# Norms between stages: sums of squares and residual adds moved to VectorE, in a two-layer hybrid trunk

## The chip, the core and the metric

The kernel runs on one core of a Trainium2 chip. The metric is the device time of one execution in microseconds (us); smaller is better. Before the change three runs took 1175.69, 1177.09 and 1179.84 us, a median of 1177.09 us.

The engines have short names throughout: PE is TensorE (matrix products), DVE is VectorE, ACT is ScalarE, POOL is GpSimd, SP is SyncE, which issues most DMAs. Each engine works through its own list of instructions in a fixed order; semaphores make it wait for others.

## The reference

The reference is a decoder trunk of two layers on 512 tokens of 1024 features. Each layer has a mixer (layer 0: dilated attention beside a state-space layer; layer 1: a gated linear recurrence) and a SwiGLU feed-forward network (FFN) with 2816 hidden columns. Every one of the four sub-layers stands between two norms:

```
def rms_norm(x, g):
    x32 = x.astype(jnp.float32)
    y = x32 * lax.rsqrt(jnp.mean(x32 * x32, axis=-1, keepdims=True) + NORM_EPS) * g.astype(jnp.float32)
    return y.astype(x.dtype)
...
        x = x + rms_norm(mix, norm_mix_post[layer])
        hn = rms_norm(x, norm_ffn_pre[layer])
        ff = swiglu(hn, ffn_w_gate[layer], ffn_w_up[layer], ffn_w_down[layer])
        x = x + rms_norm(ff, norm_ffn_post[layer])
```

So at each boundary between two sub-layers a sub-layer's output is normed and added to the residual x, and the new x is normed again, which needs the sum of its squares over the 1024 features of each token. There are three such boundaries: layer 0's mixer to its FFN, that FFN to layer 1's mixer, layer 1's mixer to its FFN.

## The kernel before

**Tiling.** Everything is held feature-major: a tile is 128 features x 512 tokens, and x is eight such tiles, `xT[0]` to `xT[7]`. A product in fp32 accuracy is made of three passes (`mm3`): operands are split into a high part (`xh`, `whi_*`) and the rest (`xl`, `wlo_*`), and high x high, high x low and low x high are added up in PSUM. Weights come from HBM as `wraw_*`; ACT rounds the high part (L240), DVE subtracts for the low part (L241).

**A boundary** is the end of `out_proj` (from L413), called three times: with the name `mo0` (first boundary, around 255 to 300 us in the trace), `fd0` (around 610 to 660) and `mo1` (around 780 to 830). In the trace `mo0` and `mo1` both show as `_mo`. The 512 tokens are done in two halves, h = 0 and 1, of 256 tokens (`HT`). For each half:

- The last products of the projection end (`op_*`), DVE adds them to the output tiles o (L527), ACT squares (L528), DVE adds the squares (L530), and PE sums them over features by one-column matmuls against a tile of ones (`cs_*`). DVE (L378) and POOL (L381, a power) make the reciprocal root `rst`/`rsy`, and PE spreads it over partitions (`bc_*`).
- Then `norm_half(h)` goes over the eight feature tiles f. For each: DVE scales o by gain and row (L494, a SCALAR_TENSOR_TENSOR, with two tensor inputs and a per-partition scalar); x is increased by it (on DVE at L498 for f < `NDVE` = 1, on POOL at L500 for the other seven); ACT makes `xh` (L501) and the square of the new x (`nsq_*`, L504); DVE makes `xl` (L489).
- The squares are summed on PE (`next_sums`, L472): for each feature tile and each block of 128 tokens one matmul with the 128 x 128 block of squares as weights and one column of ones as data, 16 in each half, accumulated in PSUM over the eight tiles (`ns_*`).

**Beside the norm** PE runs `half_cols(h)`: the first four column blocks ("heads") of the next stage, which take feature tile f as soon as its `xh` and `xl` are there: 12 products of 256 columns for each f and half (tiles `mo0b`, `f00b` and so on). The sums of the new squares are wanted only after that, in `mid()`: the next stage's products use the un-normed x, and the row of reciprocal roots is applied to their results (`rst_f`, `bc_f`, `bcs_f`).

**The order of the work.** Steps of `norm_half` are generators in a heap, taken when a clock that counts the cost of the issued products reaches their due time (`NORM_CS`, `NORM_BC`, `NORM_F` = 1000 ns for each feature tile). PE, DVE and ACT instructions of this part keep the order in which the program is written (`keep_in_program_order`, through `pe.pin` and `seq_of`); all other instructions are ordered by the framework's scheduler, so a change here can shift the order elsewhere too.

**After an FFN boundary** the feed-forward starts with column pairs that are computed with fewer products (a Strassen-like scheme). It needs sums and differences of weights (`wraw_s_f`, `wraw_t_f`, L642 to L645 on DVE) and of x (`xa_f`, `xb_f` on ACT at L660 and L661, differences `wraw_tr_f` on DVE at L664 to L667, then high parts `th_f` on ACT and low parts `tl_f` on DVE at L671 and L672). Pairs 02 to 21 go through tiles `f00b` to `f03b`; the first two of them, 02 and 03, wait for these differences. After the `fd0` boundary no such scheme follows: the next stage (`xb`, `gg`) uses plain products.

## Time and profile before

| | us |
|---|---|
| median of 3 runs | 1177.09 |
| the profiled execution | 1173.47 |
| its span in the trace | 1171.5 |
| outside the span (1173.47 - 1171.5) | 1.97 |

The profile shows one execution on the chip. A row of a group view reads: line, engine, operation, output <- inputs, count, then durations in ns (least/median/greatest) or busy time. Durations of following instructions on one engine overlap, since each starts before the one ahead has fully left the pipeline; how far apart two instructions start (the pitch) is therefore taken from start times in the timeline, and is shorter than a duration. A window row gives the busy time of each engine in a stretch of time, in us, with the number of rows, then the granted PE clock (1.00 is full speed) and DMA figures. An fp32 matmul leaves two rows in the trace, a product of the split parts one.

The busy shares over the span are 97% for PE, 75% for DVE, 54% for ACT and 5% for POOL; DVE's share in the norms and after them differs a lot from that mean.

### The profile page before, as it was taken

To read this page: it belongs to the slowest core of one execution; us is meant where nothing else is said; L and a number is where in the kernel's file an instruction comes from. 1 tells how busy PE (TensorE), PEld (TensorE's weight loads), DVE (VectorE), ACT (ScalarE), POOL (GpSimd) and SP (SyncE) were. 2 spreads that over 40 slices of the span, in tenths; PEclk is the share of its full clock that TensorE was granted. 3 is DMA by queue.
4 is the path that set the end of the run, shared out by engine and by line. 5 is a ranking of instruction groups with operands and counts; after the bars stand their busy time and mean duration, and the time that the engine had idled before them with its cause. 6 is when DMAs were issued, how large, how long until landed. Compare 5 with 4: busy or idle time off the path is not lost.

```text
span 1171.5 us, 20250 instructions
## 1 busy us (share of the span) xinstructions
PE 1134.0 (97%) x7550; PEld 1013.6 (87%) x7550; DVE 877.7 (75%) x1841; ACT 628.4 (54%) x1290; POOL 60.6 (5%) x101
## 2 busy tenths in 40 slices
PE   7899999999999999999999999999999999999997
PEld 6787766789999999988889987889999999988886
DVE  7978866557999899983445896966999899994224
ACT  6556667446755545662243469744955455582221
POOL 2000010004000000000002200004000000000001
PEclk9899899999999999999999999999999999999999
DMA  8254320430343323333340323340253343233221
GB/s 214 91 149 126 101 75 1 134 101 26 110 118 100 91 82 108 92 122 93 114 120 1 91 91 91 122 129 1 73 144 96 92 119 93 85 123 121 95 63 72
DMA packets 165273, 113.45 MB, mean 97 GB/s; under 512 B 26820, under 2 KB 141752, under 8 KB 165176
## 3 DMA queue, kind: packets, MB, share of 16 engines
q1 hardware_dynamic: 161848, 109.94, 32.1%
q10 hardware_dynamic: 3040, 2.17, 0.7%
q8 instruction: 59, 0.97, 0.4%
q14 instruction: 38, 0.31, 0.1%
q0 software_dynamic: 288, 0.07, 0.0%
HBM read 103.75 MB, written 4.19 MB: 92 GB/s over the span
## 4 chain that ended last, share of the span: by engine, by line
PE 75%; ACT 9%; DVE 7%; DMA 5%; issue 2%; POOL 1%; ACTq 0%; SPq 0%; DVEq 0%; POOLq 0%
PE fo L170 10%; PE op_fd L170 10%; PE op_mo L170 5%; PE f11b L170 4%; PE f12b L170 4%; PE f01b L170 4%; PE f00b L170 4%; PE f10b L170 4%; PE f02b L170 4%; PE qkv L170 4%; PE gg L170 3%; PE f13b L170 2%; PE f03b L170 2%; PE xbb L170 2%; PE fd0b L170 2%
## 5 line engine op out<-in xcount | busy, mean ns | idle before, releaser
L241 DVE TENSOR_TENSOR wlo_fo<-wraw_fo,whi_fo 128x512 fp32r<-128x512 f32 x44 | 30.3, 691 | 63.9 <-PE fo L170 58.3
L170 PE MATMUL op_fd<-hi_f,whi_fd 128*128 128x512 f32 (+1 forms) x200 | 73.6, 368 | 0.0
L170 PE MATMUL op_fd<-lo_f,whi_fd 128*128 128x512 f32 (+1 forms) x200 | 73.2, 366 | 0.0
L170 PE MATMUL op_fd<-hi_f,wlo_fd 128*128 128x512 f32 (+1 forms) x200 | 73.0, 368 | 0.0
L170 PE MATMUL fo<-wlo_fo,hi_f 128*128 128x512 f32 x176 | 69.5, 395 | 0.0
L170 PE MATMUL fo<-whi_fo,lo_f 128*128 128x512 f32 x176 | 69.2, 394 | 0.0
L170 PE MATMUL fo<-whi_fo,hi_f 128*128 128x512 f32 x176 | 68.9, 396 | 0.0
L240 ACT ACTIVATE whi_fo<-wraw_fo 128x512 fp32r<-128x512 f32 x44 | 27.6, 631 | 70.6 <-DMA wraw_fo<-in_ffn_w_down_dram 44.5
L241 DVE TENSOR_TENSOR wlo_fd<-wraw_fd,whi_fd 128x512 fp32r<-128x512 f32 x44 | 30.1, 691 | 46.7 <-ACT whi_fd L240 42.4
L240 ACT ACTIVATE whi_fd<-wraw_fd 128x512 fp32r<-128x512 f32 x44 | 27.4, 629 | 54.9 <-DMA wraw_fd<-in_ffn_w_down_dram 32.6
L170 PEld LDWEIGHTS op_fd<-lo_f,whi_fd 128*128 128x128 f32 x200 | 37.7, 189 | 6.9
L170 PE MATMUL qkv<-whi_qkv,xh_m 128*128 128x512 f32 x96 | 42.3, 442 | 1.4 <-DVE up L1204 1.2
L170 PEld LDWEIGHTS op_fd<-hi_f,wlo_fd 128*128 128x128 f32 x200 | 37.7, 188 | 6.7
L170 PEld LDWEIGHTS op_fd<-hi_f,whi_fd 128*128 128x128 f32 x200 | 37.7, 188 | 6.5
L170 PE MATMUL qkv<-wlo_qkv,xh_m 128*128 128x512 f32 x96 | 39.3, 409 | 2.9 <-DVE wlo_qkv L241 2.9
L170 PEld LDWEIGHTS fo<-whi_fo,lo_f 128*128 128x128 f32 x176 | 33.1, 188 | 7.8
L170 PEld LDWEIGHTS fo<-whi_fo,hi_f 128*128 128x128 f32 x176 | 33.1, 188 | 7.7
L170 PEld LDWEIGHTS fo<-wlo_fo,hi_f 128*128 128x128 f32 x176 | 33.1, 188 | 7.5
L170 PE MATMUL qkv<-whi_qkv,xl_m 128*128 128x512 f32 x96 | 39.3, 410 | 0.0
L642 DVE TENSOR_TENSOR wraw_s_f<-wraw_f,wraw_f 128x512 f32<-128x512 f32 x40 | 27.4, 686 | 12.6 <-DMA wraw_f<-in_ffn_w_up_dram 9.3
L241 DVE TENSOR_TENSOR wlo_mo<-wraw_mo,whi_mo 128x512 fp32r<-128x512 f32 x32 | 21.1, 685 | 15.3 <-ACT whi_mo L240 15.1
L643 DVE TENSOR_TENSOR wraw_t_f<-wraw_s_f,wraw_f 128x512 f32<-128x512 f32 x40 | 27.3, 684 | 6.3 <-DMA wraw_f<-in_ffn_w_gate_dram 6.3
(1975 smaller groups left out, 4301.2 us busy)
## 6 DMA issues: line engine op xcount, KB each, us to landing
wraw_f<-in_ffn_w_gate_dram SPq DMA_DIRECT2D x88, 256.0 KB, 3.2
wraw_f<-in_ffn_w_up_dram SPq DMA_DIRECT2D x88, 256.0 KB, 3.3
wraw_fd<-in_ffn_w_down_dram SPq DMA_DIRECT2D x44, 256.0 KB, 2.8
wraw_fo<-in_ffn_w_down_dram SPq DMA_DIRECT2D x44, 256.0 KB, 3.0
wraw_qkv<-in_ev_w_in_dram SPq DMA_DIRECT2D x24, 256.0 KB, 3.5
wraw_mo<-in_ev_w_out_dram SPq DMA_DIRECT2D x16, 256.0 KB, 4.7
wraw_xb<-in_od_w_in_dram SPq DMA_DIRECT2D x16, 256.0 KB, 2.8
wraw_gg<-in_od_w_in_dram SPq DMA_DIRECT2D x16, 256.0 KB, 2.9
```

What stands on the lines that cost most here:

```text
L170: self.pin(nc.tensor.matmul(o, lhsT=lhsT, rhs=rhs, start=start, stop=stop, **kw))
L240: act.activation(hi, src, AF.Copy)
L241: eng.tensor_tensor(lo, src, hi.bitcast(F32), op=ALU.subtract)
L642: dve.tensor_tensor(s1, a21, a22, op=ALU.add)
L643: dve.tensor_tensor(s2, s1, a11, op=ALU.subtract)
```

## The change

At each of the three boundaries:

- All eight residual adds of a half are done on DVE (L490 in the changed kernel); 14 POOL instructions go for each boundary, 42 in all. POOL keeps the power of L381.
- The squares of the new x are added up on DVE: ACT's squares go to four half-tiles, the first of them is the accumulator (`sq[3]`), and seven DVE additions (L494 and L498 of the changed kernel) bring the other seven in. That is 14 more DVE additions for each boundary, 28 with the residual adds.
- `next_sums` goes. PE makes four one-column matmuls for each boundary in place of 32, written after all products of the heads' first half and `drain()`, with no pinned place; the scheduler puts them.
- The low part `xl` (`split_lo`) of tile f - 1 is made in every step, right behind the scaling of tile f; before, it came one or two tiles later when POOL did the add.

```
-NDVE = 1
...
-        acc2 = [None, None]
+        acc2, total = [None, None], [None, None]
...
-        def next_sums(h, fs, q):
-            for i, f in enumerate(fs):
-                for t in range(2):
-                    c = 2 * h + t
-                    pe.pin(nc.tensor.matmul(nsum[:, c:c + 1], lhsT=q[:, i * HT + t * P:i * HT + (t + 1) * P],
-                                            rhs=ones[:, 0:1], start=(c == 0 and f == 0), stop=(f == NF - 1),
-                                            skip_group_check=True))
...
+            sq = [sb.tile([P, S], F32, tag="sqacc" if h else "sq", bufs=2, name=f"nsq_{nm}{h}{i}") for i in range(2)]
+            sq = [q[:, HS[i]] for q in sq for i in range(2)]
...
-                if late and late[0] < max(NDVE, f - 1):
+                if late:
                     split_lo()
-                if f < NDVE:
-                    seq_of(dve.tensor_tensor(xf, xf, oh, op=ALU.add))
-                else:
-                    pool.tensor_tensor(xf, xf, oh, op=ALU.add)
+                seq_of(dve.tensor_tensor(xf, xf, oh, op=ALU.add))
                 seq_of(act.activation(xh[f][:, HS[h]], xf, AF.Copy, scale=col(gname, glayer * NF + f)))
-                if f % 2 == 0:
-                    q = sb.tile([P, S], F32, tag="sqacc" if h else "sq", bufs=2, name=f"nsq_{nm}{h}{f}")
-                seq_of(act.activation(q[:, HS[f % 2]], xf, AF.Square))
+                seq_of(act.activation(sq[f % 3] if f else sq[3], xf, AF.Square))
+                if f > 1:
+                    seq_of(dve.tensor_tensor(sq[3], sq[3], sq[(f - 1) % 3], op=ALU.add))
                 late.append(f)
-                if f % 2 and f > 1:
-                    next_sums(h, (f - 3, f - 2), qlast)
-                if f % 2:
-                    qlast = q
...
-            next_sums(h, (NF - 2, NF - 1), qlast)
+            seq_of(dve.tensor_tensor(sq[3], sq[3], sq[(NF - 1) % 3], op=ALU.add))
+            total[h] = sq[3]
...
         in_order[0] = False
+        for t in range(NT):
+            pe.matmul(nsum[:, t:t + 1], lhsT=total[t // 2][:, t % 2 * P:(t % 2 + 1) * P], rhs=ones[:, 0:1],
+                      start=True, stop=True)
```

The order of each engine's list shows where this goes. The list of DVE grows from 1827 to 1917 rows, that of POOL shrinks from 107 to 65 and that of PE from 6890 to 6863 (following equal matmuls share a row).

First place, DVE in the first half of the norm at the first boundary. `o_mo` is the scaled output, `xl_mo` the low part, `xT` the residual, `nsq_mo` the squares; before, a step is one scaling and one low part:

```order
L494 SCALAR_TENSOR_TENSOR o_mo_2825<-o_mo_2825,cols,bc_mo_3123 128x256
L489 SCALAR_TENSOR_TENSOR xl_mo_2995<-xT_178,cols,xh_mo_2987 128x256
L494 SCALAR_TENSOR_TENSOR o_mo_2930<-o_mo_2930,cols,bc_mo_3123 128x256
L489 SCALAR_TENSOR_TENSOR xl_mo_2996<-xT_179,cols,xh_mo_2988 128x256
L378 TENSOR_SCALAR rst_mo_3214<-cs_mo_3209 128x2
L494 SCALAR_TENSOR_TENSOR o_mo_2932<-o_mo_2932,cols,bc_mo_3123 128x256
L489 SCALAR_TENSOR_TENSOR xl_mo_2997<-xT_180,cols,xh_mo_2989 128x256
```

The same engine and place in the changed kernel, two steps:

```order
L487 SCALAR_TENSOR_TENSOR o_mo_2825<-o_mo_2825,cols,bc_mo_3123 128x256
L482 SCALAR_TENSOR_TENSOR xl_mo_2996<-xT_179,cols,xh_mo_2988 128x256
L490 TENSOR_TENSOR xT_180<-xT_180,o_mo_2825 128x256
L494 TENSOR_TENSOR nsq_mo_3127<-nsq_mo_3127 128x256
L487 SCALAR_TENSOR_TENSOR o_mo_2930<-o_mo_2930,cols,bc_mo_3123 128x256
L482 SCALAR_TENSOR_TENSOR xl_mo_2997<-xT_180,cols,xh_mo_2989 128x256
L490 TENSOR_TENSOR xT_181<-xT_181,o_mo_2930 128x256
L494 TENSOR_TENSOR nsq_mo_3127<-nsq_mo_3127,nsq_mo_3126 128x256
```

A step has four DVE instructions where it had two, and the low part now follows by one tile.

Second place, PE at the end of the heads at the first boundary. `ns_mo` is the sum of squares, `mo0b` the heads, `f00b` the first pair. Before, such sums stand between the products, for example:

```order
L170 MATMUL mo0b_3159<-xh_mo_2993,wlo_f_1_2947 128x256
L472 MATMUL ns_mo_3002<-ones,nsq_mo_3278 128x1 x4
L170 MATMUL mo0b_3160<-xh_mo_2993,whi_f_1_2958 128x256
L170 MATMUL mo0b_3160<-xh_mo_2993,wlo_f_1_2959 128x256
L170 MATMUL mo0b_3161<-xh_mo_2993,whi_f_1_2970 128x256
```

In the changed kernel the totals of the second half stand here:

```order
L169 MATMUL mo0b_3163<-xh_mo_2993,wlo_f_1_2983 128x256
L169 MATMUL ns_mo_3002<-ones,nsq_mo_3275 128x1 x2
L169 MATMUL mo0b_3160<-xl_mo_3001,whi_f_1_2946 128x256
L169 MATMUL mo0b_3161<-xl_mo_3001,whi_f_1_2958 128x256
L169 MATMUL mo0b_3162<-xl_mo_3001,whi_f_1_2970 128x256
L169 MATMUL mo0b_3163<-xl_mo_3001,whi_f_1_2982 128x256
L169 MATMUL f00b_3606<-xh_mo_2986,whi_f02a_3492 128x256
```

Only the last four products of the heads stand behind the last sums; the totals of the first half stand at the same place of that half.

Third place, DVE some 40 rows after the norm's end at the first boundary, around the last `tl_f` (the low parts of x's differences). Before:

```order
L672 TENSOR_TENSOR tl_f_3603<-wraw_tr_f_0_3596,th_f_3602 128x512
L241 TENSOR_TENSOR wlo_f03c_3753<-wraw_s_f_0_3737,whi_f03c_3752 128x512
L241 TENSOR_TENSOR wlo_f04d_3909<-wraw_f_0_3881,whi_f04d_3908 128x512
L672 TENSOR_TENSOR tl_f_3603<-wraw_tr_f_2_3597,th_f_3602 128x256
L241 TENSOR_TENSOR wlo_f04d_3913<-wraw_f_4_3883,whi_f04d_3912 128x512
```

In the changed kernel:

```order
L662 TENSOR_TENSOR tl_f_3585<-wraw_tr_f_0_3578,th_f_3584 128x512
L633 TENSOR_TENSOR wraw_t_f_0_3869<-wraw_s_f_0_3867,wraw_f_0_3859 128x512
L634 TENSOR_TENSOR wraw_f_0_3863<-wraw_f_0_3859,wraw_f_0_3863 128x512
L240 TENSOR_TENSOR wlo_f04c_3883<-wraw_s_f_0_3867,whi_f04c_3882 128x512
L662 TENSOR_TENSOR tl_f_3567<-wraw_tr_f_2_3561,th_f_3566 128x256
L662 TENSOR_TENSOR tl_f_3585<-wraw_tr_f_2_3579,th_f_3584 128x256
L635 TENSOR_TENSOR wraw_s_f_4_3868<-wraw_f_4_3861,wraw_t_f_0_3869 128x512
```

The last `tl_f` is row 600 of DVE's list before, 48 rows behind the norm's last low part (row 552); it is row 635 after, 59 rows behind that low part (row 576). The weights of pairs 02 and 03 (`wlo_f02*`, `wlo_f03*`) now all stand ahead of it; before, `wlo_f03b` and one part each of `wlo_f03c` and `wlo_f03d` came after it.

## The prediction

> **What bounds the kernel now.** I read the page's head first, then windows of the trace around the three boundaries, then the groups of the lines that the change touches, then waits. The head says that PE is the engine to look at; the windows say where it isn't:
>
> ```profile
> span 1171.5 us, 20250 instructions
> PE 1134.0 (97%) x7550; PEld 1013.6 (87%) x7550; DVE 877.7 (75%) x1841; ACT 628.4 (54%) x1290; POOL 60.6 (5%) x101
> ```
>
> The windows are the heads with the norm at the first boundary (265 to 298.3), the FFN behind it (two rows), the second boundary and its next stage (622.3, 660), the third boundary and its FFN (793.9, 830, 860). The columns are window, length, then busy time of PE, PEld, DVE, ACT and POOL, then the granted clock:
>
> ```profile
> core 0: us, PE busy (x) PEld busy (x) DVE busy (x) ACT busy (x) POOL busy (x), PEclk, DMA share, GB/s
> 260.00:265.00 5.00, 5.00 (x31) 5.00 (x31) 2.22 (x6) 0.69 (x2) 0.71 (x1) 0.66 0.00 0
> 265.00:298.30 33.30, 32.46 (x276) 32.18 (x275) 26.55 (x64) 24.30 (x56) 13.72 (x16) 1.00 0.19 54
> 300.00:320.00 20.00, 17.93 (x145) 17.19 (x144) 20.00 (x39) 15.08 (x31) 0.00 (x0) 1.00 0.31 88
> 320.00:380.00 60.00, 60.00 (x508) 60.00 (x507) 58.91 (x120) 31.32 (x65) 0.00 (x0) 1.00 0.38 109
> 622.30:660.00 37.70, 36.90 (x314) 36.64 (x313) 24.06 (x78) 15.38 (x38) 13.49 (x16) 1.00 0.10 29
> 660.00:710.00 50.00, 50.00 (x222) 40.59 (x220) 41.55 (x72) 34.50 (x55) 0.00 (x0) 1.00 0.34 102
> 793.90:830.00 36.10, 35.34 (x298) 35.08 (x298) 26.76 (x62) 22.62 (x53) 13.54 (x16) 1.00 0.14 41
> 830.00:860.00 30.00, 28.09 (x232) 27.44 (x231) 28.39 (x57) 20.57 (x42) 0.00 (x0) 1.00 0.33 93
> 860.00:880.00 20.00, 19.00 (x156) 18.38 (x155) 20.00 (x42) 12.15 (x25) 0.00 (x0) 1.00 0.38 110
> ```
>
> Three things stand in them. Within the norms PE is the bound: it idles 0.8 us in each, DVE 6.8 to 13.6. Behind the second boundary PE is busy without a gap and DVE has 8.45 us of 50 to spare. But behind the first and the third, where the FFN's first pairs need sums of weights and of x from DVE, DVE is busy all of 300 to 320 and of 860 to 880, and it is PE that idles: 2.07 us in 300 to 320, 1.91 and 1.00 us in 830 to 880. So time saved on PE in a norm is kept at the second boundary, and at the other two only as far as DVE is ready earlier too; and the change gives DVE more work.
>
> **The matmuls removed.** The sums of squares in the first norm, first as busy time (columns: PE, PEld), then one batch in the timeline (start, length), with four products behind it:
>
> ```profile
> 265.00:298.30 33.30, 7.99 (x64) 8.14 (x64) 1.00 0.19 54
> ...
> 274.98 0.95 PE L472 MATMUL ns_mo<-ones,nsq_mo 128*128 128x1 f32 x8
> 275.79 0.48 PE L170 MATMUL mo0b<-xl_mo,whi_f 128*128 128x256 f32 x2
> 276.11 0.29 PE L170 MATMUL mo0b<-xh_mo,whi_f 128*128 128x256 f32 x1
> 276.23 0.28 PE L170 MATMUL mo0b<-xh_mo,wlo_f 128*128 128x256 f32 x1
> ```
>
> Busy time counts the ends that overlap the next product, so I go by starts: eight rows, which are four matmuls, take 275.79 - 274.98 = 0.81 us, 0.20 us each. A boundary loses 32 - 4 = 28 of them: 28 x 0.20 = 5.7 us; the busy time bounds it from above, 7.99 x 28/32 = 7.0 us. A head product takes 276.23 - 276.11 = 0.12 us, so the 12 products of a feature tile and half take 1.44 us.
>
> **The work added to DVE.** The groups are POOL's add, DVE's scaling and low part, and ACT's two steps (least/median/greatest ns); then POOL's adds of the first boundary's second half as one piece; then DVE instructions that follow each other without a gap, 256 and 512 columns wide:
>
> ```profile
> L500 POOL TENSOR_TENSOR xT<-xT,o_mo x28: 724/917/1008, 266.8 to 819.3; 128x256 f32<-128x256 f32 x28
> L494 DVE SCALAR_TENSOR_TENSOR o_mo<-o_mo,cols,bc_mo x32: 466/471/482, 263.7 to 818.7; 128x256 f32<-128x256 f32 x32
> L489 DVE SCALAR_TENSOR_TENSOR xl_mo<-xT,cols,xh_mo x32: 471/560/912, 266.6 to 823.4; 128x256 fp32r<-128x256 f32 x32
> L501 ACT ACTIVATE xh_mo<-xT,cols x32: 492/509/512, 264.7 to 822.1; 128x256 fp32r<-128x256 f32 x32
> L504 ACT ACTIVATE nsq_mo<-xT x32: 398/401/404, 265.1 to 822.5; 128x256 f32<-128x256 f32 x32
> ...
> 279.92 6.10 POOL L500 TENSOR_TENSOR xT<-xT,o_mo 128x256 f32<-128x256 f32 x7 [4.72 <-DVE o_mo L494]
> ...
> 266.22 0.47 DVE L494 SCALAR_TENSOR_TENSOR o_mo<-o_mo,cols,bc_mo 128x256 f32<-128x256 f32 x1
> 266.61 0.48 DVE L489 SCALAR_TENSOR_TENSOR xl_mo<-xT,cols,xh_mo 128x256 fp32r<-128x256 f32 x1
> ...
> 317.76 0.41 DVE L718 TENSOR_TENSOR pu_f<-pu_f 128x256 f32<-128x256 f32 x1
> 318.10 0.74 DVE L719 TENSOR_TENSOR gt_f<-f00b,bcs_f 128x256 f32<-128x256 f32 x2
> 318.76 0.68 DVE L241 TENSOR_TENSOR wlo_f03c<-wraw_s_f,whi_f03c 128x512 fp32r<-128x512 f32 x1
> 319.36 0.68 DVE L241 TENSOR_TENSOR wlo_f06a<-wraw_f,whi_f06a 128x512 fp32r<-128x512 f32 x1
> ```
>
> By starts a scaling or low part takes 266.61 - 266.22 = 0.39 us, a 256-wide add 318.10 - 317.76 = 0.34 or (318.76 - 318.10)/2 = 0.33, a 512-wide one 319.36 - 318.76 = 0.60. A boundary's 14 residual adds and 14 adds of squares cost DVE 28 x 0.335 = 9.4 us (0.335 lies between the two; with the whole duration of 0.41 us it would be 11.5 us). A step on DVE becomes 0.39 + 0.39 + 0.335 + 0.335 = 1.45 us, beside PE's 1.44 us: level. ACT's step is 0.51 + 0.40 = 0.91 us, and the chain add, xh, low part (0.41 + 0.51 + 0.47 = 1.39 us) fits into a step, so ACT and latency don't set the pace. In the second half POOL now paces the norm at 6.10/7 = 0.87 us a tile, which is faster than PE takes them; the slower DVE pace costs PE nothing as long as DVE starts a half no later than PE.
>
> DVE also gets something back. Low parts take 560 ns beside POOL's adds and 471 without: 14 x 0.09 = 1.2 us. And its waits in the norm:
>
> ```profile
> 263.75:286.20 22.45, 15.66 (x37) 0.99 0.00 1
> ...
> DVE o_mo L494 <- PE bc_mo L170: 4.5, 2, 3.1
> DVE rst_mo L378 <- PE cs_mo L170: 2.0, 1, 2.0
> DVE oacc_mo L530 <- ACT oqs_mo L528: 0.9, 1, 0.9
> DVE xl_mo L489 <- ACT xh_mo L501: 0.7, 2, 0.4
> ```
>
> The first row is DVE from the first scaling to its first FFN instruction: 22.45 - 15.66 = 6.8 us idle, mostly the 3.1 us for the second half's row and the 2.0 us for `cs`. With a fuller list DVE comes to both when they are already there; I leave it the 0.9 us for ACT and some tenths, 1.3 us together. So DVE starts on the FFN's weights later by 9.4 - 1.2 - (6.8 - 1.3) = 2.7 us at the first boundary.
>
> The Trainium skill ("SBUF — State Buffer", section "SBUF: two separate sides") calls the port pair that DVE and GpSimd share an exclusive lock, held for a whole instruction. By that, each POOL add could hold DVE up for its full 0.9 us and 14 of them give back up to 12 us, so DVE would not be late at all and the FFN boundaries would go toward the first rival below. The rows bear out a small part: the scaling, whose row operand lies in PSUM, stays at 471, the low part loses 0.09, and DVE works on through POOL's 6.10 us.
>
> **What becomes of it, boundary by boundary.** *Second* (`fd0`): PE-bound before and behind, so the 5.7 us are kept: -5.7 (-7.0 to -5; a later DVE costs nothing there with 8.45 us spare). *First*: PE ends the heads some 6 to 8 us earlier, and meets a DVE list that runs 2.7 us late. What DVE does last there for pairs 02 and 03 is the last `tl_f`. Before, it started as the first row below shows (a step of the chain that ended last), and the last product of the two pairs as the second:
>
> ```profile
> 311.49 0.34 DVE tl_f L672
> ...
> 323.75 0.28 PE L170 MATMUL f02b<-xh_mo,wlo_f03c 128*128 128x256 f32 x1
> ```
>
> After, DVE's list from the first scaling to that `tl_f` (rows 509 to 635) adds up, with 0.39 and 0.335 for the short ones and 0.60 for the 512-wide, to 52.35 us: 263.75 + 1.3 + 52.35 = 317.4 us. It comes later, but behind the two last `tl_f` PE has only 32 products of these pairs left, 3.8 us: 321.2 us. Before, PE had done ten products of pair 04 by 323.87, so its equal is 323.87 - 1.2 = 322.7. Gain 1.4 us; between 4 (DVE a little less full than I count) and a loss of 2.7 (the whole delay handed on). *Third*: the same count gives about 1 us of gain, for the same reason; -3.5 to +1.5. From there on DVE and PE run as before, PE full (60.00 of 60.00 in 320 to 380).
>
> POOL's 42 adds cost nothing today except through ACT's waits; their removal is in the above. The four totals (0.85 us) stand ahead of the last four head products and wait for DVE's last add of squares, which follows the last `xh` by one ACT step and one add, within the products' time; on SP and POOL's DMA queues nothing is moved past anything.
>
> Sum: -5.7 - 1.4 - 1.0 = -8.1 us. The profiled execution goes from 1173.47 to 1165.4 us; it lies 3.6 us below the median of three runs, so on the median the forecast is 1177.09 - 8.1 = 1169.0 us, with a range of its own of 1163 to 1176.
>
> **The rivals.** *All of the PE time is kept.* If DVE's list at the FFN boundaries has more slack than its 20.00 of 20.00 shows (it works ahead for later pairs), three times 5.7 us come off: -17.1, 1160.0 us. For it: the FFN's weights for later pairs stand between. Against: PE already waits there. Chance 0.13.
>
> *DVE hands its delay on, refilled.* The 2.7 us are lost at both FFN boundaries: 2 x 2.7 - 5.7 = -0.3, 1176.8 us, no difference. For it: DVE 100% busy. Chance 0.17.
>
> *DVE hands on the whole added work: slower.* If DVE still waits for `bc` and `cs` because the steps and PE's order come at the same times as before, nothing is refilled, and it is 9.4 - 1.2 = 8.2 us late at both FFN boundaries: 2 x 8.2 - 5.7 = +10.7, 1187.8 us. It decides from a delay of (5.7 + 3.5)/2 = 4.6 us on. For it: the order of engines' lists is fixed, and one late ACT or DMA there stops everything behind it. Against: the waits of 3.1 and 2.0 us are for work that PE reaches earlier now. Chance 0.13.
>
> *PE's clock falls.* At the first boundary, after, PE is through with what it can do (some 27 products, 3.3 us, and the row) at about 294 us and the next product wants a `wlo_f03a` that DVE delivers at 265.0 + 33.3 = 298.3: a pause of 4 us. The window 260 to 265 shows what a drop costs: at a clock of 0.66 it loses 5 x 0.34 = 1.7 us. Ahead of it PE had waited for this at most:
>
> ```profile
> PE cs_mo L170 <- DVE oacc_mo L530: 0.7, 1, 0.7
> ```
>
> Two such drops: -8.1 + 3.4 = -4.7, 1172.4 us. Against it: the pauses behind today's boundaries, 2 to 3 us in all, leave the clock at 1.00. The Trainium skill ("TensorE: Matmul & The Clock Gate", section "HAM oscillation — how this bites in real kernels") puts the limit at idle gaps over some 3.4 us, which a pause of 4 us would pass; the row of 0.7 us shows a drop after a far shorter wait, so the trace does not bear the limit out. Chance 0.07.
>
> That the change doesn't do what it says I rule out: the lists show 42 POOL rows gone and 90 DVE rows more.
>
> **How the numbers follow.** The forecast has 0.50. About 0.3% (3.5 us) is what a measurement of this kernel can tell from no change, that is, below 1173.6 or above 1180.6. Faster: nine tenths of the forecast (0.45), the first rival (0.13) and half of the clock's (0.04): 0.62. Slower: the third rival and a little of the second's upper end: 0.15. Same: the rest, 0.23. The range takes in the full gain below (1159) and the refilled delay with 1 us of scatter above (1178), and leaves out the slower case.
>
> **What would show it.** Right: no POOL adds; DVE without a wait over 1 us in the norms; the heads at 298.3 ending near 291 to 292, those at 660 near 654; DVE busy and PE with waits on `wlo_f03*`, `tl_f` between 292 and 320 that sum to some 5 us more than before. Wrong: DVE waits of 2 to 3 us left in the norm, the heads ending less than 4 us earlier, waits on `xl` or `ns` inside the heads, or PE at 321 in the same place as before or further back.

## The result, and the profile after

The changed kernel takes 1184.32 us in the median of six runs (1181.39 to 1187.04), the kernel before 1177.3 in six runs beside it (1173.81 to 1179.84): a ratio of 1.0078 with a 95% interval of 1.0054 to 1.0102. It is slower by 0.8%, where 1169.0 us was forecast. The profiled execution took 1181.39 us.

The head of the page of the changed kernel, against that of before:

```profile
span 1179.6 us, 19906 instructions
PE 1125.4 (95%) x7382; PEld 1002.5 (85%) x7382; DVE 900.9 (76%) x1925; ACT 633.3 (54%) x1290; POOL 28.8 (2%) x59
```

PE is busy for 8.6 us less and the span is 8.1 us longer. To see where, cut the span at the first row of reciprocal roots (`bc_*`) of each boundary: three stages follow it. First the kernel before, then the changed one (window, length, busy PE, PEld, DVE, ACT, POOL, clock, DMA):

```profile
262.65:622.32 359.67, 355.91 (x2546) 334.01 (x2546) 278.83 (x543) 184.12 (x369) 14.42 (x17) 1.00 0.33 96
622.32:793.29 170.97, 169.30 (x938) 145.82 (x937) 129.64 (x251) 108.46 (x190) 14.20 (x17) 1.00 0.30 90
793.29:1171.50 378.21, 366.65 (x2561) 339.84 (x2559) 276.90 (x534) 182.16 (x371) 18.58 (x32) 1.00 0.30 91
```

```profile
261.58:626.12 364.54, 355.39 (x2489) 331.10 (x2489) 287.63 (x571) 185.94 (x369) 4.66 (x3) 0.99 0.32 95
626.12:798.02 171.90, 164.97 (x882) 140.63 (x881) 136.91 (x279) 108.84 (x190) 2.41 (x3) 0.98 0.30 89
798.02:1179.60 381.58, 364.63 (x2505) 337.83 (x2503) 283.75 (x562) 185.12 (x371) 8.35 (x18) 0.99 0.30 90
```

The stages are 4.9, 0.9 and 3.4 us longer (with 1.1 us less ahead of them: 8.1). The last column but two shows that busy time is not work here: the clock is below 1.00 in all three. So I split each stage further, in windows of 1 us: *idle* is length less PE busy, *lost to the clock* is busy time times (1 - clock), and what is left is *work* at full clock. In us, changed kernel against before:

| stage | work | idle | lost to the clock | length |
|---|---|---|---|---|
| first row to second | 351.4 (355.2) | 9.2 (3.8) | 4.0 (0.8) | +4.9 |
| second to third | 163.0 (169.3) | 6.9 (1.7) | 2.0 (0.0) | +0.9 |
| third to the end | 360.0 (366.7) | 16.9 (11.5) | 4.7 (0.0) | +3.4 |
| sum of changes | -16.8 | +16.0 | +9.9 | +9.1 |

In this pair of profiles PE's work fell by 16.8 us, which is what the matmuls removed were priced at (3 x 5.7 = 17.1). PE's waits ate 16.0 of it, and the clock took 9.9 more. A second profile of the changed kernel (e9 below) has -14.5, +18.5 and +6.3 against the same profile of before, so figures of single profiles of one kernel lie 2 to 4 us apart.

DVE around the first boundary's norm: its window from the first scaling to its first L633 behind the norm, and the two longest of its waits in it:

```profile
262.68:289.80 27.12, 24.06 (x66) 0.98 0.10 30
...
DVE wlo_f03a L240 <- ACT whi_f03a L239: 2.0, 1, 2.0
DVE oacc_mo L517 <- ACT oqs_mo L515: 0.9, 1, 0.9
```

Against 22.45 us and 15.66 busy before: 8.4 us more work, and 3.06 us idle left instead of the 1.3 counted on. The waits for the second half's row and for `cs` are gone, as forecast. The largest piece is a new wait on ACT, whose list now has a weight of pair 03 ahead of the last tile's `xh`, and that weight waits for a DMA. Before, the first weight of pair 03 stood far behind, as the last row below shows:

```profile
288.52 0.63 ACT L239 ACTIVATE whi_f03a<-wraw_f 128x512 fp32r<-128x512 f32 x1 [2.23 <-DMA wraw_f<-in_ffn_w_gate_dram]
289.06 0.49 ACT L491 ACTIVATE xh_mo<-xT,cols 128x256 fp32r<-128x256 f32 x1
...
296.47 0.62 ACT L240 ACTIVATE whi_f03a<-wraw_f 128x512 fp32r<-128x512 f32 x1
```

The same wait, of 2.4 us for `whi_f13a`, stands at the third boundary.

What PE waits for longest behind the heads, in the window 286 to 335 and in 820 to 875, and then the longest of the kernel before, in 298 to 335 and 830 to 880:

```profile
PE f00b L169 <- ACT xb_f L651: 1.7, 1, 1.7
PE f02b L169 <- ACT xh_mo L661: 1.5, 1, 1.5
PE f03b L169 <- DVE ut_f L714: 1.4, 1, 1.4
...
PE f11b L169 <- DVE pu_f L710: 2.4, 1, 2.4
PE f10b L169 <- ACT pu_f L695: 2.3, 2, 1.6
...
PE f01b L170 <- ACT pu_f L707: 1.2, 1, 1.2
...
PE f11b L170 <- DVE tl_f L672: 1.0, 1, 1.0
```

These are waits for preparation on ACT and DVE. Behind the second boundary there is one new wait, of 4.9 us, 93 us behind the boundary's first row. PE's timeline around it (start, length; 512 columns each):

```profile
718.34 0.39 PE L169 MATMUL rg<-cl,whi_rg 128*128 128x512 f32 x1
718.58 0.40 PE L169 MATMUL rg<-ch,wlo_rg 128*128 128x512 f32 x1
723.87 0.80 PE L169 MATMUL rg<-ch,whi_rg 128*128 128x512 f32 x1 [4.90 <-ACT gr L1542]
724.47 0.63 PE L169 MATMUL rg<-cl,whi_rg 128*128 128x512 f32 x1
724.89 0.63 PE L169 MATMUL rg<-ch,wlo_rg 128*128 128x512 f32 x1
```

The gate products wait for a PSUM bank that ACT reads (L1542). Before the pause they start 0.24 us apart, behind it 0.42: the clock has fallen. The granted clock behind this pause, and behind two places of the third boundary (window, length, PE busy, clock):

```profile
723.50:728.00 4.50, 4.13 (x10) 0.52 0.08 23
837.00:844.00 7.00, 6.24 (x30) 0.51 0.14 40
867.50:871.50 4.00, 3.68 (x18) 0.57 0.00 1
```

The second of these falls has no long pause ahead of it: PE was idle for 1.5 of the 4.06 us before 837.06, in waits of 1.0 us and less. The first begins while PE still waits: PE stops at 718.97, the clock is down from 721.01 to 727.84, and PE goes on at 723.87.

```profile
718.97:721.01 2.04, 0.00 (x1) 1.00 0.00 0
721.01:727.84 6.83, 3.97 (x9) 0.50 0.03 10
727.84:731.00 3.16, 3.16 (x15) 1.00 0.51 150
```

### The profile page after: what moved, and what is told of

The parts are those of the page before. It is cut to its first block, busy times and chain, and to the rows that moved or that the text cites. A ratio compares the mean times of both kernels' runs of the same rounds, so it can differ in the third digit from the quotient of the medians.

```text
span 1179.6 us, 19906 instructions
## 1 busy us (share of the span) xinstructions
PE 1125.4 (95%) x7382; PEld 1002.5 (85%) x7382; DVE 900.9 (76%) x1925; ACT 633.3 (54%) x1290; POOL 28.8 (2%) x59
## 3 DMA queue, kind: packets, MB, share of 16 engines
q1 hardware_dynamic: 161848, 109.94, 31.7%
## 4 chain that ended last, share of the span: by engine, by line
PE 78%; DVE 9%; ACT 6%; DMA 4%; issue 2%; POOL 0%; ACTq 0%; DVEq 0%; POOLq 0%; SPq 0%
PE fo L169 10%; PE op_fd L169 10%; PE op_mo L169 7%; PE qkv L169 5%; PE f12b L169 5%; PE f10b L169 4%; PE f11b L169 4%; PE f02b L169 4%; PE f00b L169 4%; PE f01b L169 4%; PE gg L169 3%; PE f13b L169 2%; PE f03b L169 2%; PE xbb L169 2%; PE rg L169 1%
## 5 line engine op out<-in xcount | busy, mean ns | idle before, releaser
L239 ACT ACTIVATE whi_fd<-wraw_fd 128x512 fp32r<-128x512 f32 x44 | 27.4, 629 | 54.4 <-DMA wraw_fd<-in_ffn_w_down_dram 32.0
L604 DVE TENSOR_TENSOR hh_f<-ut_f,gt_f 128x512 f32<-128x512 f32 x44 | 30.0, 684 | 2.1 <-ACT gt_f L602 2.1
```

Source lines behind the costliest of these rows:

```text
L239: act.activation(hi, src, AF.Copy)
L604: dve.tensor_tensor(h, ut, gt, op=ALU.mult)
```

## The experiments

The theory formed from this: the next stage waits for the later of two things (the "two clocks" of the expectations, which are not PE's clock): the heads on PE, and the end of the norm with the preparation behind it on DVE and ACT; the change advances the first and delays the second. The rivals: it is the added waits inside the norm, an order of the lists made worse by the scheduler, or the clock. The first is small: near the end of the heads PE waits 1.3 us for `xh` at the second and at the third boundary, 2.6 of the 16.0 us. Times of one group of runs are beside runs of the kernel before on the same chip. Work, idle and lost to the clock are PE's account of the one profiled run, summed from the first row to the end. The last column is the mean granted clock of all timed runs, of this kernel / of before beside it; 0.001 of it is about 1.2 us of the span.

| run | us / before | ratio, 95% interval | work | idle | lost to the clock | mean clock |
|---|---|---|---|---|---|---|
| before | | | 891.2 | 17.0 | 0.8 | 0.992 (its profile) |
| changed kernel, first profile | 1184.32 / 1177.3 | 1.0054 to 1.0102 | 874.4 | 33.0 | 10.7 | 0.9835 |
| e9_after_again | 1184.35 / 1178.83 | 1.0030 to 1.0073 | 876.7 | 35.5 | 7.1 | 0.9853 / 0.9880 |
| e1_pool_adds | 1179.15 / 1179.42 | 0.9961 to 1.0001 | 876.6 | 33.9 | 4.5 | 0.9874 / 0.9877 |
| e2_adds_only | 1189.81 / 1179.42 | 1.0051 to 1.0117 | 892.1 | 24.7 | 6.6 | 0.9836 / 0.9877 |
| e3_fd_only | 1178.05 / 1179.42 | 0.9973 to 1.0021 | 885.0 | 22.2 | 6.7 | 0.9876 / 0.9877 |
| e4_mo_only | 1182.19 / 1179.42 | 1.0006 to 1.0038 | 884.6 | 30.0 | 1.5 | 0.9855 / 0.9877 |
| e5_row_late | 1187.27 / 1176.52 | 1.0059 to 1.0126 | 893.3 | 21.3 | 9.1 | 0.9854 / 0.9891 |
| e6_first_half | 1180.05 / 1176.52 | 0.9991 to 1.0045 | 885.1 | 23.8 | 2.4 | 0.9862 / 0.9891 |
| e7_fd_gates | 1175.51 / 1176.52 | 0.9969 to 1.0014 | 885.1 | 21.7 | 6.5 | 0.9887 / 0.9891 |
| e8_fd_pool | 1174.93 / 1176.52 | 0.9959 to 1.0006 | 886.2 | 19.6 | 8.5 | 0.9885 / 0.9891 |
| e10_row_early | 1184.31 / 1178.83 | 1.0025 to 1.0069 | 886.8 | 22.4 | 10.2 | 0.9822 / 0.9880 |
| e11_fd_row_late | 1178.52 / 1178.83 | 0.9981 to 1.0020 | 890.5 | 19.1 | 6.9 | 0.9890 / 0.9880 |
| e12_few_sums | 1161.11 / 1178.83 | 0.9829 to 0.9880 | 875.5 | 17.4 | 3.1 | 0.9870 / 0.9880 |
| e13_round_sums | 1169.47 / 1178.01 | 0.9908 to 0.9954 | 879.5 | 24.8 | 2.9 | 0.9900 / 0.9892 |
| e14_no_sq_adds | 1177.52 / 1178.01 | 0.9986 to 1.0021 | 871.5 | 30.4 | 8.2 | 0.9827 / 0.9892 |
| e15_fill21 | 1178.44 / 1178.11 | 0.9985 to 1.0026 | 882.8 | 27.4 | 3.2 | 0.9896 / 0.9888 |
| e16_fill10 | 1178.34, one run | | 879.4 | 32.6 | 5.0 | 0.991 |
| e17_fill15 | 1185.04, one run | | 881.6 | 32.0 | 3.4 | 0.986 |

The account of one profile and the clock of all runs don't say quite the same. The profiled run of before was a lucky one, with a clock of 0.992 where 118 timed runs of that kernel have 0.9885 in the mean. In those runs time goes with the clock (correlation -0.88): the quarter with the lowest clock takes 1182.1 us, the quarter with the highest 1174.6. And in e9's group the clocks differ by 0.0027, some 3 of the changed kernel's 5.5 us, not 9.9.

**The adds given back to POOL (e1).** Against the changed kernel: squares still summed on DVE, one step later; residual adds on POOL as before.

```
-                if late:
+                if late and late[0] < max(1, f - 1):
                     split_lo()
-                seq_of(dve.tensor_tensor(xf, xf, oh, op=ALU.add))
+                if f > 2:
+                    seq_of(dve.tensor_tensor(sq[3], sq[3], sq[(f - 2) % 3], op=ALU.add))
+                if f < 1:
+                    seq_of(dve.tensor_tensor(xf, xf, oh, op=ALU.add))
+                else:
+                    pool.tensor_tensor(xf, xf, oh, op=ALU.add)
```

> At all three boundaries the sums of squares go to VectorE as in the change, but GpSimd keeps its 14 residual adds a boundary, so VectorE gets 14 adds a boundary (4.7 us) and not 28 (9.4 us). Theory 1, the added VectorE work is handed on to the FFN's first pairs: with 4.7 us, of which 5 us of waits in the norm can take up nearly all, the FFN boundaries lose nothing and the heads keep their 3 to 5 us; the whole comes out 5 to 13 us under the kernel before, 1164 to 1172 us. Theory 2, any change of the heads' length makes the scheduler put out worse lists behind the norm, whatever the engine: still slower than before, 1180 us or more.

Neither: 1179.15 us, the time of before. DVE's adds of squares, and POOL's adds of x in the timeline:

```profile
L491 DVE TENSOR_TENSOR nsq_mo<-nsq_mo,nsq_mo x12: 415/955/961, 270.2 to 825.6; 128x256 f32<-128x256 f32 x12
...
285.37 0.92 POOL L495 TENSOR_TENSOR xT<-xT,o_mo 128x256 f32<-128x256 f32 x1 [0.75 <-DVE o_mo L487]
287.05 0.91 POOL L495 TENSOR_TENSOR xT<-xT,o_mo 128x256 f32<-128x256 f32 x1 [0.75 <-DVE o_mo L487]
```

An add of two tiles in SBUF takes DVE 955 ns beside POOL's adds, and 0.41 alone (L494 of the changed kernel). With POOL's 0.92 the two take turns, and the step becomes 287.05 - 285.37 = 1.68 us where PE needs 1.44. The Trainium skill ("SBUF — State Buffer", section "SBUF: two separate sides") says that a DVE instruction with two SBUF inputs and a GpSimd one that reads SBUF exclude each other for a whole instruction; these rows agree. My dismissal of it went by the scaling, with its row in PSUM, and by the low part, which has two inputs in SBUF and lost only 0.09 us; for the adds it was wrong.

**The adds alone on DVE, sums on PE as before (e2).** Against the kernel before:

```
-NDVE = 1
+NDVE = 8
...
-                if late and late[0] < max(NDVE, f - 1):
+                if late and late[0] < f:
```

> At all three boundaries the 14 residual adds go from GpSimd to VectorE, each followed by the low part one tile later as in the change, but TensorE keeps its 32 sums of squares. Theory 1 (added VectorE work is handed on): half of the added work, 4.7 us a boundary, no saving on TensorE; with the waits refilled within 2 us of the kernel before, 1175 to 1180 us. Theory 2 (lists get worse only when the heads get shorter): no difference, 1177 us. Slower by 5 us or more would say that the residual adds on VectorE are the dear part.

1.0084: half of DVE's added work, with nothing taken from PE, costs some 10 us. In its profile PE's work is that of before, its idle time is 7.7 us more and its loss to the clock 5.8. (The clocks of the timed runs differ by 0.0041, some 5 us.) ACT's list doesn't have pair 03's weight ahead of pair 02's here, so the added adds cost time without that order too.

**The change at one kind of boundary (e3, e4).** In e3 `new = nm[0] == "f"` chooses the new form at the second boundary alone, in e4 `new = nm[0] == "m"` at the first and third.

```
+        new = nm[0] == "f"
...
-                seq_of(dve.tensor_tensor(xf, xf, oh, op=ALU.add))
+                if new or f < NDVE:
+                    seq_of(dve.tensor_tensor(xf, xf, oh, op=ALU.add))
+                else:
+                    pool.tensor_tensor(xf, xf, oh, op=ALU.add)
```

> The whole change at the second boundary alone (FFN to layer 1's mixer), the other two as before. The trace of the changed kernel shows the heads 4.7 us shorter there and a wait of 4.9 us of TensorE in layer 1's gates, where two banks are taken early by the order of its list. That order is the same in this kernel. If the wait belongs to this boundary: 0 to 1 us under the kernel before, 1176 to 1177 us. If it came from lateness carried over from the first boundary: 4 to 5 us under, 1172 to 1173 us.

> The whole change at the first and third boundary (mixer to FFN) alone, the second as before. If the loss stands at the FFN boundaries, where the trace of the changed kernel shows pairs 02 and 03 ending 9 us further back than the heads, this kernel is at least as slow as the whole change: 8 to 11 us over the kernel before, 1185 to 1188 us. If the loss were mainly in layer 1's mixer: 2 to 5 us over, 1179 to 1182 us.

The second boundary alone brings nothing (0.9997), the FFN boundaries alone lose a little (1.0022). So the -5.7 us that seemed safest are not there. The two ratios together make +0.2%, the whole change +0.5 to +0.8%: against e9's 1.0052 that gap lies within the intervals, against the first 1.0078 it doesn't, and it stays open.

**Nothing added, only a later row (e5, e11).** The kernel before, with the second half's row put 28 products (3.4 us) later into PE's list, at the FFN boundaries in e5, at the second in e11.

```
-            yield NORM_BC[h]
+            yield NORM_BC[h] + (3000.0 if h and nm[0] == "m" else 0.0)
```

> The kernel before with one number changed: at the first and third boundary the second half's row of reciprocal roots is issued 28 products (3.4 us) later in TensorE's list. No instruction is added on any engine, and the heads still have their tiles in time. Theory H, handover: what the FFN's first pairs cost is set by the moment at which the norm's second half ends on ScalarE and VectorE, since both are full from there on until the pairs run; then 3 us are lost at each of the two boundaries, 5 to 7 us over the kernel before, 0.4 to 0.6% slower. Theory L, load: only VectorE's added work counts; none is added, so no difference.

> The kernel before, with the second half's row 28 products (3.4 us) later at the second boundary alone. As I forecast, TensorE is the bound behind that boundary: no difference, since the heads still have their tiles in time. Theory H for this boundary too (convolution on VectorE and gates on ScalarE start when the second half ends, and TensorE has no wait in the gates only because it is late itself): 3 to 5 us over the kernel before.

In e5 DVE waits for the row, and ACT's weight of pair 02 waits behind the norm (27.2 us behind the first row, before 23.4):

```profile
DVE o_mo L494 <- PE bc_mo L170: 6.9, 2, 5.5
...
293.00 0.63 ACT L240 ACTIVATE whi_f02a<-wraw_f 128x512 fp32r<-128x512 f32 x1 [0.36 <-POOL xT L500]
```

1.0093, or 11 us at two boundaries, without an instruction more and with the heads' products the same. That is more than the 5 to 7 us expected; the clock of its runs is lower by 0.0037, some 4 us. So a norm that ends late costs the FFN boundaries by itself. At the second boundary the same delay costs nothing (1.0000): the norm ended 3.4 us later, the next stage's first `xc` 1.7, so some slack lies there.

**The first half alone (e6).** The new form for `h == 0` at the FFN boundaries (`half = nm[0] == "m"`), the old one for `h == 1`.

```
+            new = half and not h
...
+                    pe.matmul(nsum[:, t:t + 1], lhsT=sq[3][:, t * P:(t + 1) * P], rhs=ones[:, 0:1],
+                              start=(t == 0), stop=True, skip_group_check=True)
```

> At the first and third boundary only the first half of the norm is changed (adds and sums of squares on VectorE, two totals on TensorE); the second half stays as before, with GpSimd's adds at 0.87 us a tile and TensorE's sums. The second boundary is as before. VectorE gets half of the added work, 14 adds (4.7 us) a boundary, all in the first half, where it waited. Theory H: the second half ends no later than before, so nothing is lost, and 14 matmuls (2.8 us) less in the heads bring 0 to 2 us a boundary: 0 to 4 us under the kernel before. Theory L: half of the loss at the FFN boundaries stays, 1 to 4 us over the kernel before.

1.0018 with an interval across 1: inconclusive.

**Is it the order of PE's list (e7)? Or DVE's share (e8)?** e7 is e3 with the products of `gates(2)` and `gates(3)` kept in the order of the program (`pe_order`), e8 the form of e1 at the second boundary alone.

```
+        pe_order[0] = True
         gates(2, last["sqrt"])
         gates(3, last["sqrt"])
+        pe_order[0] = False
```

> The whole change at the second boundary alone, and in layer 1's mixer the gate products of blocks 2 and 3 keep the order in which they are written, so that no bank is taken early. If the wait of 4.9 us in the gates was the scheduler's order and not the norm's: the 4.7 us of the heads are kept, 3.5 to 5.5 us under the kernel before. If the wait has another cause (late x, ScalarE's table loads): as without the pinning, within 1 us of the kernel before.

> At the second boundary alone the sums of squares go to VectorE, with GpSimd keeping the residual adds; the other boundaries are as before. VectorE's additions beside GpSimd's took 0.95 us in place of 0.41 in the earlier run of this form, so the norm's step gets 1.66 us long, but VectorE has spare time behind this boundary, and the gates' order is the usual one there. Heads 3 to 4 us shorter, 2.5 to 4 us under the kernel before. If the slow step starves the heads: within 1 us of the kernel before.

e7 took the wait on `rg` from 4.9 to 3.1 us, and no time was won (0.9991), so the order there is a part of its cause at most:

```profile
PE rg L170 <- ACT gr L1569: 3.2, 2, 3.1
```

In e8 the norm's last low part on DVE comes 30.9 us behind the first row, where the changed kernel has 31.7 and before 27.8, and the pause on `rg` is 1.9 us. The stage has 168.1 us, 2.9 less than before: there part of PE's gain is kept. In time it is 0.9983, interval across 1.

**The row earlier (e10).** If a late norm costs, an early one should pay.

```
-            yield NORM_BC[h]
+            yield NORM_BC[h] - (1800.0 if h and nm[0] == "m" else 0.0)
...
-                yield NORM_F
+                yield 700.0 if nm[0] == "m" else NORM_F
```

> The kernel before with two due times changed at the first and third boundary: steps of a half every 700 instead of 1000, and the second half's row 1800 earlier, which puts that row 11 products (1.3 us) further ahead in TensorE's list. No instruction is added or removed. Theory H (the end of the norm's second half sets what follows): 1.3 to 2 us gained at each of the two boundaries, 2.5 to 4 us under the kernel before. If something else sets it (loads, or the products themselves): no difference.

A miss: 1.0047. The norm's last low part came 2.1 and 3.5 us earlier, but at the first boundary the heads' last product started at +38.0 instead of +35.5, ACT's weights of pair 02 moved behind the last tile in its list, and PE paused for 3.3 us. The clock fell too (window, PE busy, clock):

```profile
270.00:280.00 10.00, 9.42 (x69) 0.83 0.01 2
320.00:330.00 10.00, 10.00 (x74) 0.84 0.29 84
```

So the delay is not a single dial; what is earlier in one list is later in another. And the timed runs have a clock of 0.9822 against 0.9880, some 7 us, which is as much as the whole loss: whether an earlier row pays is not settled by this run.

**PE relieved, DVE not loaded (e12).** The kernel before with the sums of two of the eight feature tiles; those of the other six are left out.

```
-                if f % 2 and f > 1:
-                    next_sums(h, (f - 3, f - 2), qlast)
+                if f == 3:
+                    next_sums(h, (0, 1), qlast)
...
-            next_sums(h, (NF - 2, NF - 1), qlast)
```

> The kernel before with the sums of squares of the first two feature tiles only, 8 of 32 matmuls a boundary; the other tiles' squares are left out of the norm's sum. VectorE, ScalarE and GpSimd do what they did. TensorE is 24 x 0.2 = 4.8 us a boundary shorter, and the second half's row comes some 2.4 us earlier, since the first half's sums no longer stand ahead of it. If TensorE's time counts in full: 14 us under the kernel before. Theory H: only the row's 2.4 us count, 2 to 3.5 us a boundary, 6 to 10 us under.

-17 us (0.9855), as much as the work that PE lost (15.7 us in the account), with idle time the same (+0.4). PE time taken out of the norms pays in full here, where DVE has no more to do and the norm ends earlier as well: with fewer sums ahead of the second half's row, the last low part comes 4.4, 3.0 and 5.1 us earlier than before. So e12 advances both things that the next stage waits for; it does not show what PE's time alone is worth. PE and DVE are both nearly full behind the third boundary (window; PE, PEld, DVE, ACT, POOL, clock):

```profile
830.00:863.00 33.00, 32.76 (x276) 32.56 (x275) 32.09 (x65) 19.53 (x40) 0.00 (x0) 1.00 0.40 112
```

**DVE relieved (e14).** The changed kernel without its 14 adds of squares for each boundary; the total is that of one tile, the squares of the other seven are left out.

```
-                if f > 1:
-                    seq_of(dve.tensor_tensor(sq[3], sq[3], sq[(f - 1) % 3], op=ALU.add))
...
-            seq_of(dve.tensor_tensor(sq[3], sq[3], sq[(NF - 1) % 3], op=ALU.add))
```

> The changed kernel without VectorE's 14 additions of squares a boundary: the totals are of one feature tile each, the other squares are left out of the norm's sum. TensorE's list is that of the changed kernel; VectorE has the 14 residual adds alone, a step of 1.12 us in place of 1.45. Two-clock theory: the heads end as in the changed kernel, the second half ends 2 to 2.5 us earlier, and the FFN's first pairs and the gates come 2 to 2.5 us earlier at each boundary: 6 to 8 us under the changed kernel, 0 to 3 us from the kernel before on either side. If the order of the lists and not the additions is the cause: no difference from the changed kernel, 6 to 9 us over the kernel before.

1.0003: the loss against before is gone, with PE's matmuls unchanged. But nothing is gained, for PE now waits for ACT. The pause at the gates is still there, and at both FFN boundaries PE waits some 4 us for ACT's weight of pair 03 (13):

```profile
PE rg L169 <- ACT gr L1539: 4.8, 1, 4.8
...
PE f00b L169 <- ACT whi_f03a L239: 4.0, 1, 4.0
...
PE f10b L169 <- ACT whi_f13a L239: 3.9, 1, 3.9
```

PE lost 8.2 us to the clock in this profile, and over the timed runs the clock is 0.9827 against 0.9892, some 8 us.

**Cheaper sums on PE (e13).** The kernel before, with the squares rounded to fp32r as ACT writes them, so that the sums are of rounded squares and a matmul takes one pass (two columns, 1 and 0, in place of one).

```
+    ones_r = sb.tile([P, 2], F32R, name="ones_r")
...
-                    pe.pin(nc.tensor.matmul(nsum[:, c:c + 1], lhsT=q[:, i * HT + t * P:i * HT + (t + 1) * P],
-                                            rhs=ones[:, 0:1], start=(c == 0 and f == 0), stop=(f == NF - 1),
+                    pe.pin(nc.tensor.matmul(nsum[:, 2 * c:2 * c + 2], lhsT=q[:, i * HT + t * P:i * HT + (t + 1) * P],
+                                            rhs=ones_r, start=(c == 0 and f == 0), stop=(f == NF - 1),
...
-                    q = sb.tile([P, S], F32, tag="sqacc" if h else "sq", bufs=2, name=f"nsq_{nm}{h}{f}")
+                    q = sb.tile([P, S], F32R, tag="sqacc" if h else "sq", bufs=2, name=f"nsq_{nm}{h}{f}")
```

> The kernel before with its 32 sums of squares a boundary kept on TensorE, but ScalarE writes the squares rounded as it rounds the products' high parts, so that a sum is one pass and not two. VectorE and GpSimd do what they did. A sum should take about 0.1 us in place of 0.2: heads 3.2 us shorter at each boundary, and the second half's row 1.2 us earlier. Two-clock theory (what follows a boundary waits for the later of TensorE's heads and the end of the norm plus the preparation on VectorE and ScalarE): both come earlier, so 2.5 to 3.2 us are kept at each boundary, 7 to 10 us under the kernel before. If only a large cut as in the run with few sums pays, or the rounding costs ScalarE time: 0 to 3 us under.

0.9931: 8.5 us faster than before, and the only version with the whole sums that beats both kernels clearly. Its sums in the first norm (window; PE, PEld), then four of them and the next product in the timeline:

```profile
265.00:298.30 33.30, 4.62 (x32) 4.63 (x32) 1.00 0.23 64
...
273.67 0.58 PE L477 MATMUL ns_mo<-ones_r,nsq_mo 128*128 128x2 f32 x4
274.12 0.72 PE L170 MATMUL mo0b<-xl_mo,whi_f 128*128 128x256 f32 x4
```

(274.12 - 273.67)/4 = 0.11 us a sum where the fp32 one took 0.20, and DVE does the same in the norms. The norm's last low part comes 4.3, 0.7 and 2.9 us earlier too. Not all of it is kept: in the profile PE's work is 11.7 us less and its idle time 7.8 more.

**The change once more (e9).**

> The changed kernel once more, so that its ratio stands beside the others of this set on one chip. Parts measured apart gave 0.22% slower (first and third boundary alone) and no difference (second alone), the whole 0.78% slower; if the parts simply add up, it comes out at 0.1 to 0.4% slower here, else at 0.6 to 0.9%.

1.0052, where up to 1.004 was expected if the parts add up and 1.006 or more if they don't: it lies between, on another chip, with the same waits (4.9 on `rg`, 2.3 on `pu_f`) and the same falls of the clock behind them.

**Do the pauses make the clock fall (e15, e16, e17)?** Counted by PE's idle time ahead of an instruction, all profiles together have 14 pauses of 2.0 us or more behind 255 us (2.33 to 4.91; 13 of them in the profiles ahead of e15, where the expectation below says fourteen). With each the clock falls to half, and stays there for 2.9 to 6.1 us behind the pause. That is only an order of events. These three put products with a tile of zeros ahead of the 4.9 us pause, added to the bank just finished, 21, 10 or 15 of them; the result stays what it was.

```
+                    for j in range(21 if fill else 0):
+                        pe.matmul(b, lhsT=zero_r, rhs=ch[0], start=False, stop=(j == 21 - 1))
```

> The changed kernel with 21 extra products in the second boundary's next stage, ahead of the pause of 4.9 us in which PE waited for a bank that ACT's gr reads: they multiply a tile of zeros and are added to the bank of the product ahead of the pause, so they add nothing to the result and 21 x 0.235 = 4.9 us to PE's list. Theory one, the clock falls because PE paused: the wait on gr is under 1 us, the gates' products behind it start 0.23 us apart and not 0.43, no clock loss behind it where the changed kernel's two profiles lost 2.0 and 2.5 us, and the stage from the second to the third boundary is about 2 us shorter than their 171.9 and 173.4 us. The time is some 2 us below the changed kernel's 1184.3, ratio to before about 1.004. Rival, the clock falls here for another reason (chance, or the products themselves): the window of 5 us behind the place shows a granted clock of 0.5 to 0.6 all the same, and the stage stays at 172 to 173 us.

> As the run with 21, with 10 such products of zeros: the pause should be 4.9 - 10 x 0.235 = 2.5 us. In the profiles so far all fourteen pauses of PE of 2.0 us and more behind the first boundary's start were followed by some 4 us of a clock near half. If about 2 us is the limit, the clock falls behind this pause too, for some 4 us, and costs 1.6 to 2 us. The Trainium skill (TensorE: Matmul & The Clock Gate, section HAM oscillation) puts the limit at 3.4 us; by that the clock stays at 1.00 here.

> As the run with 21, with 15 such products of zeros: the pause should be 4.9 - 15 x 0.235 = 1.4 us. With a limit of about 2 us the clock stays at 1.00 behind it; if it falls for another reason, it is 0.5 to 0.6 for some 4 us again.

With 21 there is no pause, and the products behind start 0.24 us apart (timeline, then the window behind with its clock; so too in the two fences after this):

```profile
717.95 5.06 PE L169 MATMUL rg<-ch,zero_r 128*128 128x512 f32 x21
722.85 0.40 PE L169 MATMUL rg<-ch,whi_rg 128*128 128x512 f32 x1
723.09 0.39 PE L169 MATMUL rg<-cl,whi_rg 128*128 128x512 f32 x1
...
722.90:728.00 5.10, 5.10 (x22) 1.00 0.01 3
```

With 10, a pause of 2.57 us, and the clock falls; with 15, one of 1.41, and it doesn't:

```profile
722.60 0.80 PE L169 MATMUL rg<-ch,whi_rg 128*128 128x512 f32 x1 [2.57 <-ACT gr L1550]
723.20 0.63 PE L169 MATMUL rg<-cl,whi_rg 128*128 128x512 f32 x1
...
722.50:726.00 3.50, 3.40 (x8) 0.51 0.02 5
```

```profile
727.54 0.50 PE L169 MATMUL rg<-ch,whi_rg 128*128 128x512 f32 x1 [1.41 <-ACT gr L1550]
727.87 0.40 PE L169 MATMUL rg<-cl,whi_rg 128*128 128x512 f32 x1
...
727.50:732.00 4.50, 4.46 (x19) 1.00 0.40 115
```

So the pause is the cause here. The profiles put its limit at this place between 1.9 and 2.6 us: pauses on `rg` of 4.9 (three profiles), 4.8, 3.1 and 2.6 us came with a fall; two of 1.9 us, one of 1.4 and the place without a pause (e15) did not. It is no fixed limit: of all 57 pauses of 1.3 to 2.0 us behind 255 us, 16 came with a fall. The Trainium skill ("TensorE: Matmul & The Clock Gate", section "HAM oscillation — how this bites in real kernels") puts it at idle gaps over some 3.4 us; by that the 2.57 us would have cost nothing, and the row says otherwise. In time, e15 came out at 1.0005, some 0.5% below e9's ratio, where I expected 0.2%. The clock of its runs is 0.9896 where e9 has 0.9853, some 5 of the 5.9 us between their medians. The stage in question gave 1.0 to 2.5 us in the profile; the third stage was 3.4 us shorter too, most of it in what it lost to the clock (1.6 us against 4.7); the 2.4 us wait on `pu_f` is not in it (from the end of that mixer on, the order of the lists differs). How much belongs to which stays open.

## Why the prediction was wrong

- **The work removed: right.** 17.1 us for three boundaries were worked out, 16.8 measured (14.5 in e9's profile). The heads end 5.3, 4.7 and 4.8 us earlier, counted from the boundary's first row.
- **The work added to DVE: right in size.** 9.4 - 1.2 = 8.2 us against 8.4 (the window leaves out the last add and holds one FFN low part instead). The trace has 84 DVE instructions more, 28 for each boundary; the 90 rows of the list were not 90 instructions. DVE's 52.35 us up to the last `tl_f` were right as well, with 52.99 busy.
- **"DVE starts on the FFN's weights later by 2.7 us": the step that failed first.** The first low part for pair 02 came at +29.6 us behind the first row instead of +24.2, and at the third boundary at +32.7 instead of +27.7: 5.4 and 5.0. I let DVE's waits refill down to 1.3 us, and the old ones did; but a new one of 2.0 us came (2.4 at the third boundary), for ACT's weight that waited for a DMA. The rest of the difference is instructions that now stand ahead of that low part. I had counted ACT's step (0.91 us) and not the FFN weights that stand between the steps in its list. The delay passes the third rival's "4.6 us on", though not for the reason given there: the waits for `bc` and `cs` did refill. In e5 a delay of 3.8 and 4.8 us at the same low part cost 11 us, some 4 of it by the clock, without any added work.
- **"Gain 1.4 us" and "about 1 us" at the FFN boundaries: follow from it.** PE's work fell by 3.8 and 6.7 us there, its idle time rose by 5.4 and 5.4. At the first boundary the last `tl_f` started at 318.3 us where 317.4 was counted, and the last product of pairs 02 and 03 at 323.78, where before had 323.75 with ten products of pair 04 already done. The same rows showed DVE full before (20.00 of 20.00), and that was the right thing to look at; I priced the delay by a count of one list. The place of pair 03's weight in ACT's list was chosen by the scheduler, and no run put it back: how much of the loss at these two boundaries is the order's stays open.
- **"Second: PE-bound before and behind, so the 5.7 us are kept": failed, and I was surest of it.** PE full in 660 to 710 does not say that PE would be full if it came 5 us earlier. DVE's 8.45 us to spare did not bring the gates forward: the norm's last low part came 3.9 us later (+31.7 against +27.8), and ACT's gate step that PE waits for started where it had (+97.0 against +96.8). The gain came out as a pause of 4.9 us, 93 us behind the boundary's first row. What sets this pause is only argued: in e14 PE's first gate product comes 2.6 us earlier and ACT's step 2.9, and the pause stays at 4.8, so DVE's adds of squares alone don't make it.
- **The clock: named, and far too small.** "Two such drops", 3.4 us and a chance of 0.07. It took 9.9 us more than in before's profile, and by the clocks of the timed runs some 3 us in e9's group. I took 2 to 3 us of pauses in sum as harmless; e15 to e17 show that a single long pause is enough, and two of the changed kernel's four falls stand behind shorter waits (1.74 us ahead of 294.34; 1.0 and less ahead of 837.06). In the profiles the clock is what makes the change slower and not only useless (work -16.8, idle +16.0, clock +9.9); in the timed runs of e9 it is about half of the loss, and e15 is level with before once one pause is filled.
- **What the sum was set against.** The profiled run of before had lost only 0.8 us to the clock in these stages; its clock of 0.992 is above the 0.9885 of the 118 timed runs, and other profiles of the same norms lose more (below), so the median lies higher. Single profiles of one list differ by several us in a stage; the verdicts above rest on the timed ratios with their intervals, and the account tells where the time lies.

## What to carry to other kernels

Time taken off the busiest engine is worth what the engines that feed the next stage can deliver sooner; if the same edit loads one of them inside the stage that ends last there, count the delay at its last output, with every foreign instruction in every feeder's list. Price a new pause of the matrix engine twice when it is longer than about 2 us: here the clock fell with every one of these, at a cost of some 1.5 to 3 us. Before moving work to another engine, look for a cheaper form where it stands: one pass in place of two gave more here than moving the sums away.

## What the runs showed of the hardware

- A pause of PE of 2.57 us was followed by 3.4 us at half the clock, one of 1.41 was not (rows above). Over all profiles, falls came with 14 of 14 pauses of 2.33 us and more, 16 of 57 of 1.3 to 2.0 us, and 3 of 41 of 1.0 to 1.3 us.
- In the clock records of all 19 traces the granted clock is 1.00 or 0.50, and within a trace it changes only at multiples of 3.41 us from its first change: a fall that lies whole in the record lasts 3.41 us, 6.83 (as in 721.01 to 727.84 above) or a higher multiple. Whether a pause of 1.3 to 2.0 us is followed by a fall may hang on where it lies between two such moments; no run tried that.
- The clock also falls without such a pause, in norms where fp32 sums of one column stand between the products. In the window 3 to 27 us behind each boundary's first row, 9 of 23 such norms lost 1.6 to 6.8 us (33.6 us together, 1.5 a norm), and none of 32 norms in which the sums were few, in one pass or on DVE (e6's two mixed norms are left out). A run of e8 in the first norm, where PE's longest wait ahead was 1.1 us:

```profile
269.50:284.00 14.50, 14.50 (x74) 0.53 0.00 1
```

  Why was not tried; it may be a part of the scatter of the kernel before, which goes with the clock (1171.25 to 1185.87 us over the 118 runs).
- Two-input adds on DVE beside POOL's adds take 955 ns in place of 0.41 us (e1); a scaling with its row in PSUM and the low part hardly noticed them before.
